# A fused seven-stage network on one core: later index products, two copies on ScalarE's DMA queue, a causal mask by addition, roots by log and exp, low weight parts on GpSimd, all in the sparse attention stage

## The chip, the cores and the metric

The kernel runs on one core of a Trainium2 chip. The core has a matrix engine (TensorE, PE in the profile), a vector engine (VectorE, DVE), an activation engine (ScalarE, ACT), a general engine (GpSimd, POOL) and a sequencer that here only starts transfers (SyncE, SP). Each engine takes its instructions strictly in program order; an instruction waits on semaphores for what it reads and for the buffer that it writes. ACT, POOL and SP can each start DMA transfers. The metric is the device time of one execution in microseconds (us), lower is better.

## The reference, cut to what matters

A sequence of 512 tokens with 1024 features goes through seven stages: ffn1, mix, ffn2, dsa, ffn3, conv, ffn4. Only dsa, a sparse attention, is touched here:

```python
proj = h @ w_in                       # q 16 heads, k and v 4 heads, qi 8 heads, ki 1, wi 8, head size 64
q = _rope(_rmsnorm(q, q_norm_g), positions);  k = _rope(_rmsnorm(k, k_norm_g), positions)
qi = _rope(qi, positions)
ki = _rope(_layernorm(ki, ...))       # one index key per token
# for each block of 128 queries:
score = einsum(relu(einsum(qi, ki)), wi * scale)      # sum over the 8 index heads
score = where(key <= query, score, -inf)              # causal
_, sel = top_k(score, 128)                            # 128 keys for each query
o = softmax(q . k[sel] * scale) . v[sel]
return o @ w_out
```

## The kernel before, in words

Every float32 matrix product is made of three products of rounded parts (high times high, high times low, low times high; L461 to L463). A weight tile is loaded by SP as `raw` (1 MB, L101), rounded by ACT to `whi` (L124, a cast of 128x1024), and its low part `wlo` is a subtraction (L126, 128x1024) by DVE, or by POOL for every second tile while `W.pool_lo` is true, and for every tile while it is 2. One projection of 128 output rows is a block of 24 matmuls.

The stage dsa_block runs so. First the index projections: ki with the 8 weights wi, then QI0 to QI3. Each goes through `rope`: `t` gets the halves of the raw tile swapped by DMAs of SP (L1464, L1465), POOL multiplies raw by cos (L1466) and t by sin (L1469), DVE adds (L1472). ki (tile U4, 64 partitions) is then copied to its upper 64 partitions by one DMA (L1525), since two index heads are computed at a time, one in each half of the array.

Next k0, k1, v0, v1 and q0 to q7 are projected, one block after the other. After each block stands a "step" (L470): it runs the functions that were put off (`deferred`), and one round of the generator `beside_q`. A round of it does, in this order: `weighed` (ACT's Relu of the last index products, L1567, and DVE's weighted sum over heads, L1569 and L1571; at head 7 the causal part by POOL's affine_select, L1575), `select` (rounds of top-8 search: MAX, L1605, and MATCH_REPLACE, L1606; 16 rounds for each query block j = 1, 2, 3, on 256, 384 and 512 columns), the sums of q's norms (`add`, L1681; its `rest` is DVE's L1686, POOL's power -0.5 in L1687 and four small POOL operations, L1689 to L1692), stages of attention "units", and `some_products` (the next index products on PE, L1555). `some_products` does nothing until `ready` is set, which `last` in evac_ki does by a deferred function.

A unit is a pair of heads of one set of query blocks: 8 units for j = 0 and 1, 8 for j = 2, 8 for j = 3. Its steps are scores (L1748), the masked reduction with the selection (DVE, L1765), Exp (ACT), division (DVE L1774, POOL L1776), transposes (PE L1785), copies (ACT L1796), values (PE L1807). When all q blocks are done a second loop runs the remaining units, one iteration each, with `select(1.4)` (two rounds) in each iteration while selection lasts. Units of j = 3 need sel[3], which one DVE instruction (L1609, 512 columns) writes when the 16 rounds of j = 3 are done.

DVE's and ACT's order is thus the order in which this Python code runs; nothing is rescheduled. Names of tiles: U4 ki, U0 to U3 the index queries, U14 to U21 q, F0 and F5 the raw k, F1 to F3 the index scores, `sq` the Relu results (two buffers), A and B the PSUM banks, `ada_w` q's raw tile, `col` small columns.

Of the kernel before, what the change touches and what calls it, by code (L numbers as in the profile page):

```python
# [18 lines left out]
P = 128  # L19
# [218 lines left out]
def body(ctx: ExitStack, tc: tile.TileContext, A: dict, consts: bass.AP, out: bass.AP,  # L238
# [1214 lines left out]
    def dsa_block(layer):  # L1453
# [5 lines left out]

        def rope(out, raw, n=P, then=None):  # L1460

            t = tmp()[0:n]
            for a in range(0, n, 64):
                nc.sync.dma_start(t[a:a + 32], raw[a + 32:a + 64])  # L1464
                nc.sync.dma_start(t[a + 32:a + 64], raw[a:a + 32])  # L1465
            nc.gpsimd.tensor_tensor(out, raw, cos[0:n], op=ALU.mult)  # L1466

# [20 lines left out]
        def evac_qi(c, ps):  # L1488
            raw = tmp()
            nc.scalar.copy(raw, ps)  # L1490
            rope(QI[c], raw)

# [3 lines left out]
        def evac_ki(c, ps):  # L1496
# [4 lines left out]
            def rest():  # L1501
# [11 lines left out]
                def more():  # L1513
# [10 lines left out]
                    def last():  # L1524
                        nc.sync.dma_start(ki[HALF[1]], ki[HALF[0]])  # L1525
                        deferred.append(lambda: ready.append(True))

                    rope(ki[HALF[0]], z, 64, last)

# [30 lines left out]
        def weighed():  # L1560

            for j, h, ps in parts:
# [5 lines left out]
                if h == 0:  # L1568
                    nc.vector.tensor_scalar(sc[:, 0:n], t[:, 0:n], w, None, op0=ALU.mult)  # L1569
                else:  # L1570
                    nc.vector.scalar_tensor_tensor(sc[:, 0:n], t[:, 0:n], w, sc[:, 0:n], op0=ALU.mult,  # L1571
                                                   op1=ALU.add)
                if h == 7:
                    dg = sc[:, P * j:n]
                    nc.gpsimd.affine_select(dg, dg, pattern=[[-1, P]], base=0, channel_multiplier=1,  # L1575
                                            compare_op=ALU.is_ge, fill=NEG)
                    whole.append(j)
# [50 lines left out]
        def evac_k(c, ps):  # L1628
# [4 lines left out]
            def swapped(t):  # L1633
                for i in range(2):
                    nc.sync.dma_start(KS[t][HALF[i]], kraw[t][HALF[1 - i]])

# [34 lines left out]
        def evac_q(c, ps):  # L1671
# [6 lines left out]
            def add():  # L1678
# [5 lines left out]
                def rest():  # L1684
                    v, y, z = colt((P, 8)), colt((P, 8)), colt((P, 8))
                    nc.vector.tensor_scalar(v, both, 1.0 / 64, EPS, op0=ALU.mult, op1=ALU.add)  # L1686
                    nc.gpsimd.tensor_tensor(y, v, mhalf, op=ALU.pow)  # L1687

# [175 lines left out]
        side_work.append(beside_q())  # L1864
        W.pool_lo = True
        proj_T("dsa", 2, H, evac_k)
        proj_T("dsa", 2, H, evac_v)
        proj_T("dsa", 8, H, evac_q)
        side_work.clear()
# [4 lines left out]
        go(1)  # L1874
        while adds:
            adds.pop(0)()
        phase[0] = False
        now = at[0]
        while at[6] < len(units):
            go(5, now - 4)  # L1880
            go(6)
            go(3, now - 2)
            go(0)
            go(2, now)
            now += 1
# [157 lines left out]
```

## Time and profile before

| | us |
|---|---|
| median of three runs (lowest to highest) | 2710.66 (2710.25 to 2711.5) |
| the profiled execution, its own time | 2706.65 |
| its span in the trace | 2704.9 |
| PE busy, share of the span | 2625.6, 97% |
| DVE busy | 1389.4, 51% |
| ACT busy | 908.7, 34% |
| POOL busy | 554.0, 20% |
| mean granted clock of PE | 0.985 |

The profile is of one execution. Busy time is that of instructions that do work; transfers and semaphores are not in it. A clock of 1.00 is 2.4 GHz, 0.50 is 1.2 GHz. The stage dsa covers about 1465 to 1740 us of the span.

### The profile page before, as it was taken

What the parts mean: (1) busy time and instruction counts of PE and PEld (TensorE: products, weight loads), DVE (VectorE), ACT (ScalarE), POOL (GpSimd) and SP (SyncE); (2) the same over time, 40 slices, a digit from 0 to 9 for tenths busy, and PEclk for the clock granted to TensorE, in tenths of its full rate; (3) what the DMA queues carried; (4) which work ended last, traced back from release to release, by engine and by line L of the source; (5) the groups of instructions that cost most, each with busy time, mean ns of one, the idle gap of its engine ahead of it and who ended that gap; (6) DMA issues with size and microseconds to landing.
All of it is one profiled execution on the core that took longest, in us unless ns stands there. A gap on an engine that the chain in (4) does not pass through costs nothing.

```text
span 2704.9 us, 32602 instructions
## 1 busy us (share of the span) xinstructions
PE 2625.6 (97%) x13020; PEld 2186.4 (81%) x13020; DVE 1389.4 (51%) x2060; ACT 908.7 (34%) x1447; POOL 554.0 (20%) x577
## 2 busy tenths in 40 slices
PE   8999999999999999999998787999999999999999
PEld 7888889888777788888887665888888888888887
DVE  5545566365637454665556587463333454533332
ACT  4322233323344433423223334642222332322222
POOL 3211234254112111412123346320000200200000
PEclk9999999999999999999999887999999999999999
DMA  6555443222221234256543221022232322232322
GB/s 186 160 177 184 150 144 115 63 78 79 85 72 63 78 100 135 90 156 201 184 147 123 75 74 59 2 93 91 97 109 71 117 94 94 79 105 82 109 86 71
DMA packets 256875, 289.11 MB, mean 107 GB/s; under 512 B 10004, under 2 KB 238916, under 8 KB 256724
## 3 DMA queue, kind: packets, MB, share of 16 engines
q1 hardware_dynamic: 244596, 235.57, 27.6%
q0 software_dynamic: 10496, 50.95, 6.0%
q8 instruction: 103, 1.69, 0.2%
q10 hardware_dynamic: 1632, 0.52, 0.1%
q14 instruction: 48, 0.39, 0.0%
HBM read 278.59 MB, written 4.19 MB: 105 GB/s over the span
## 4 chain that ended last, share of the span: by engine, by line
PE 88%; DVE 7%; POOL 1%; ACT 1%; issue 1%; DMA 1%; SPq 0%; DVEq 0%; ACTq 0%; POOLq 0%
PE mm L461 25%; PE mm L462 25%; PE mm L463 25%; PE mm L544 2%; PE mm L657 1%; PE mm L658 1%; PE mm L659 1%; DVE col L1605 1%; DVE F L1606 1%; PE B L1136 1%; DVE X L810 1%; DVE L L696 1%; PE mm L1748 1%; PE mm L1807 1%; PE A L1279 1%
## 5 line engine op out<-in xcount | busy, mean ns | idle before, releaser
L461 PE MATMUL mm<-H,whi 128*128 128x512 f32 (+1 forms) x2360 | 902.5, 382 | 0.0
L463 PE MATMUL mm<-H,wlo 128*128 128x512 f32 (+1 forms) x2360 | 894.1, 379 | 0.9 <-DVE wlo L126 0.9
L462 PE MATMUL mm<-L,whi 128*128 128x512 f32 (+1 forms) x2360 | 894.5, 379 | 0.3 <-DVE L L696 0.3
L126 DVE TENSOR_TENSOR wlo<-raw,whi 128x1024 fp32r<-128x1024 f32 (+3 forms) x432 | 503.6, 1166 | 547.8 <-ACT whi L124 546.1
L124 ACT CAST whi<-raw 128x1024 fp32r<-128x1024 f32 (+3 forms) x460 | 444.6, 968 | 408.8 <-PE mm L462 329.0
L461 PEld LDWEIGHTS mm<-H,whi 128*128 128x128 f32 x2360 | 445.9, 189 | 91.5 <-issue 10.7
L463 PEld LDWEIGHTS mm<-H,wlo 128*128 128x128 f32 x2360 | 445.4, 189 | 84.8 <-DVE wlo L126 1.6
L462 PEld LDWEIGHTS mm<-L,whi 128*128 128x128 f32 x2360 | 445.7, 189 | 82.1 <-DVE L L696 1.0
L461 PE MATMUL mm<-U,whi 128*128 128x512 f32 (+1 forms) x804 | 312.4, 389 | 0.0
L463 PE MATMUL mm<-U,wlo 128*128 128x512 f32 (+1 forms) x804 | 310.8, 387 | 0.0
L462 PE MATMUL mm<-U,whi 128*128 128x512 f32 (+1 forms) x804 | 310.7, 386 | 0.0
L413 POOL TENSOR_TENSOR acc<-acc,sq 128x512 f32<-128x512 f32 (+1 forms) x74 | 92.8, 1254 | 640.8 <-ACT sq L400 640.0
L670 ACT CAST U<-t 128x512 fp32r<-128x512 f32 x104 | 64.6, 621 | 406.9 <-POOL t L759 194.2
L461 PEld LDWEIGHTS mm<-U,whi 128*128 128x128 f32 x804 | 151.0, 188 | 33.5 <-issue 3.3
L463 PEld LDWEIGHTS mm<-U,wlo 128*128 128x128 f32 x804 | 151.0, 188 | 30.8
L462 PEld LDWEIGHTS mm<-U,whi 128*128 128x128 f32 x804 | 151.0, 188 | 30.1
L671 DVE TENSOR_TENSOR U<-t,U 128x512 fp32r<-128x512 f32 x104 | 72.0, 693 | 134.2 <-ACT U L670 134.2
L882 POOL DMA_DIRECT2D ada_w<-in_ada_w_dram x128 | 71.3, 557 | 281.1 <-DVE wide L906 221.1
L906 DVE SCALAR_TENSOR_TENSOR wide<-ada_w,csilu,wide 128x768 f32<-128x768 f32 x112 | 115.0, 1027 | 15.9 <-DMA ada_w<-in_ada_w_dram 15.9
L126 POOL TENSOR_TENSOR wlo<-raw,whi 128x1024 fp32r<-128x1024 f32 (+1 forms) x28 | 66.2, 2363 | 256.8 <-ACT whi L124 255.1
L757 DVE TENSOR_TENSOR t<-t,mm 128x512 f32<-128x512 f32 x88 | 60.3, 685 | 110.9 <-PE mm L463 110.8
L759 POOL TENSOR_TENSOR t<-t,R 128x512 f32<-128x512 f32 x44 | 56.4, 1283 | 217.5 <-DVE t L757 210.4
(394 smaller groups left out, 2807.9 us busy)
## 6 DMA issues: line engine op xcount, KB each, us to landing
ada_w<-in_ada_w_dram POOLq DMA_DIRECT2D x128, 384.0 KB, 3.6
raw<-in_ffn_w_up_dram SPq DMA_DIRECT2D x44, 1024.0 KB
raw<-in_ffn_w_gate_dram SPq DMA_DIRECT2D x43, 1024.0 KB
raw<-in_w_in_dram SPq DMA_DIRECT2D x30, 1024.0 KB
raw<-in_ffn_w_down_dram SPq DMA_DIRECT2D x32, 768.0 KB
raw<-in_ffn_w_down_dram SPq DMA_DIRECT2D x32, 640.0 KB
raw<-in_w_in_dram SPq DMA_DIRECT2D x24, 512.0 KB
raw<-in_conv_w_in_dram SPq DMA_DIRECT2D x12, 1024.0 KB
```

What stands on the lines that cost most here:

```text
L124: nc.scalar.copy(hi, raw)
L126: e.tensor_tensor(lo, raw, hi.bitcast(F32), op=ALU.subtract)
L413: (eng or nc.vector).tensor_tensor(self.acc[:, c], self.acc[:, c], sq[:, c], op=ALU.add)
L461: nc.tensor.matmul(ps, whi, hhi, start=start, stop=False)
L462: nc.tensor.matmul(ps, whi, hlo, start=False, stop=False)
L463: nc.tensor.matmul(ps, wlo, hhi, start=False, stop=stop)
L670: nc.scalar.copy(hi, src)
L671: nc.vector.tensor_tensor(lo, src, hi.bitcast(F32), op=ALU.subtract)
L757: nc.vector.tensor_tensor(s, s, ps, op=ALU.mult)
L759: nc.gpsimd.tensor_tensor(s, s, R, op=ALU.mult)
L882: nc.gpsimd.dma_start(loaded[i], A["ada_w_2"][layer, k * P:(k + 1) * P, 768 * cg:768 * (cg + 1)])
L906: nc.vector.scalar_tensor_tensor(acc, w, csilu[:, k:k + 1], acc, op0=ALU.mult, op1=ALU.add)
```

## The change

Eight edits, all in dsa_block:

1. `rope` takes an engine for the cos product. For the four index queries and ki it is DVE, before it was POOL.
2. ki's copy to the upper half is started from ACT's queue, before from SP's.
3. `ready` is set one step later, so all ten calls for index products come one projection block later.
4. The causal part is no longer POOL's affine_select after head 7. The first head's product is split: the columns before the diagonal block by a TENSOR_SCALAR, the 128 of the diagonal block by a SCALAR_TENSOR_TENSOR that also adds a triangular mask.
5. k's four half copies (`swapped`) are started from ACT's queue, before from SP's.
6. The power -0.5 of q's norms is ACT's Ln and Exp on 128x8, before one POOL operation.
7. While k and v are projected all low parts are made by POOL. Tiles are prepared ahead, so these are the weights of q0 to q3.
8. After the last projection the sum of q7's norm is taken up in the second loop, before it stood ahead of the loop.

```diff
-        def rope(out, raw, n=P, then=None):
+        def rope(out, raw, n=P, then=None, e=nc.gpsimd):
...
-            nc.gpsimd.tensor_tensor(out, raw, cos[0:n], op=ALU.mult)
+            e.tensor_tensor(out, raw, cos[0:n], op=ALU.mult)
...
-            rope(QI[c], raw)
+            rope(QI[c], raw, e=nc.vector)
...
-                        nc.sync.dma_start(ki[HALF[1]], ki[HALF[0]])
-                        deferred.append(lambda: ready.append(True))
+                        nc.scalar.dma_start(ki[HALF[1]], ki[HALF[0]])
+                        deferred.append(lambda: deferred.append(lambda: ready.append(True)))
-                    rope(ki[HALF[0]], z, 64, last)
+                    rope(ki[HALF[0]], z, 64, last, nc.vector)
...
-                    nc.vector.tensor_scalar(sc[:, 0:n], t[:, 0:n], w, None, op0=ALU.mult)
+                    nc.vector.tensor_scalar(sc[:, 0:P * j], t[:, 0:P * j], w, None, op0=ALU.mult)
+                    nc.vector.scalar_tensor_tensor(sc[:, P * j:n], t[:, P * j:n], w, masks[:, 896:1024], op0=ALU.mult,
+                                                   op1=ALU.add)
...
-                    dg = sc[:, P * j:n]
-                    nc.gpsimd.affine_select(dg, dg, pattern=[[-1, P]], base=0, channel_multiplier=1,
-                                            compare_op=ALU.is_ge, fill=NEG)
...
-                    nc.sync.dma_start(KS[t][HALF[i]], kraw[t][HALF[1 - i]])
+                    nc.scalar.dma_start(KS[t][HALF[i]], kraw[t][HALF[1 - i]])
...
-                    nc.gpsimd.tensor_tensor(y, v, mhalf, op=ALU.pow)
+                    act(y, v, AF.Ln)
+                    act(y, y, AF.Exp, scale=-0.5)
...
-        W.pool_lo = True
+        W.pool_lo = 2
         proj_T("dsa", 2, H, evac_k)
         proj_T("dsa", 2, H, evac_v)
+        W.pool_lo = True
         proj_T("dsa", 8, H, evac_q)
...
-        while adds:
-            adds.pop(0)()
         phase[0] = False
...
             go(0)
+            if adds:
+                adds.pop(0)()
+                banks.clear()
+                step()
             go(2, now)
```

Three places show how instructions move. The first is PE's order after the projection of k0 (matmuls into the tile `mm`); L1555 are the first index products, of ki (U_1184) with QI0 and QI1 (U_1180, U_1181). Before, they stand right behind k0, and k1 (mm_11407) follows:

```order
L462 MATMUL mm_11365<-L_1164_10900,whi_11231 128x512
L463 MATMUL mm_11365<-H_1163_10899,wlo_11232 128x512
L1555 MATMUL A_11392<-U_1184_10974,U_1180_10970 128x256 x2
L1555 MATMUL A_11392<-U_1184_10974,U_1181_10971 128x256 x2
L461 MATMUL mm_11407<-H_1149_10885,whi_11275 128x512
L462 MATMUL mm_11407<-L_1150_10886,whi_11275 128x512
```

Now the 24 matmuls of k1 (mm_11401) and the first sum of k's norms (L1659) stand ahead of them, and v0 (mm_11441) follows:

```order
L462 MATMUL mm_11401<-L_1164_10900,whi_11275 128x512
L463 MATMUL mm_11401<-H_1163_10899,wlo_11276 128x512
L1659 MATMUL B_11351<-acc_11393,dsa_consts 20x512
L1555 MATMUL A_11428<-U_1184_10974,U_1180_10970 128x256 x2
L1555 MATMUL A_11428<-U_1184_10974,U_1181_10971 128x256 x2
L461 MATMUL mm_11441<-H_1149_10885,whi_11302 128x512
L462 MATMUL mm_11441<-L_1150_10886,whi_11302 128x512
```

So PE has one block more to do before it needs ki's upper half and QI0, QI1. The second place is POOL from the start of the index queries' rotation on; `rc` is cos, `rs` sin, U_1180 to U_1183 the index queries, U_1184 ki. Before:

```order
L1466 TENSOR_TENSOR U_1180_10970<-t_11223,rc_8270 128x512
L1466 TENSOR_TENSOR U_1184_10974<-t_11260,rc_8270 64x512
L1469 TENSOR_TENSOR t_11225<-t_11225,rs_8271 128x512
L1466 TENSOR_TENSOR U_1181_10971<-t_11267,rc_8270 128x512
L1469 TENSOR_TENSOR t_11262<-t_11262,rs_8271 64x512
L1469 TENSOR_TENSOR t_11269<-t_11269,rs_8271 128x512
L1466 TENSOR_TENSOR U_1182_10972<-t_11294,rc_8270 128x512
L1469 TENSOR_TENSOR t_11296<-t_11296,rs_8271 128x512
L1466 TENSOR_TENSOR U_1183_10973<-t_11337,rc_8270 128x512
L1469 TENSOR_TENSOR t_11339<-t_11339,rs_8271 128x512
L126 TENSOR_TENSOR wlo_11455<-raw_11235,whi_11454 128x1024
L1575 AFFINE_SELECT F_1238_11393<-F_1238_11393 128x128
```

Now:

```order
L1469 TENSOR_TENSOR t_11225<-t_11225,rs_8271 128x512
L1469 TENSOR_TENSOR t_11262<-t_11262,rs_8271 64x512
L1469 TENSOR_TENSOR t_11269<-t_11269,rs_8271 128x512
L1469 TENSOR_TENSOR t_11296<-t_11296,rs_8271 128x512
L1469 TENSOR_TENSOR t_11339<-t_11339,rs_8271 128x512
L126 TENSOR_TENSOR wlo_11396<-raw_11235,whi_11395 128x1024
L126 TENSOR_TENSOR wlo_11438<-raw_11235,whi_11437 128x1024
L126 TENSOR_TENSOR wlo_11488<-raw_11306,whi_11487 128x1024
L126 TENSOR_TENSOR wlo_11571<-raw_11306,whi_11570 128x1024
```

The five cos products are gone from POOL, and four low parts stand right behind the last sin product, where one stood before. The third place is ACT after q2's block. Before, the Relu of the index scores (`sq`) follows the cast:

```order
L1673 ACTIVATE ada_w_11828<-mm_11755,cB 128x512
L1675 ACTIVATE acc_11830<-mm_11755 128x512
L124 CAST whi_11838<-raw_11529 128x1024
L1567 ACTIVATE sq_11886<-A_11822 128x512
L1567 ACTIVATE sq_11889<-A_11822 128x512
```

Now k's copies (U_1185, U_1186 from the raw k in F_1223, F_1224) and the Ln and Exp (on `col`) stand between them:

```order
L1672 ACTIVATE ada_w_11798<-mm_11743,cB 128x512
L1674 ACTIVATE acc_11800<-mm_11743 128x512
L124 CAST whi_11808<-raw_11491 128x1024
L1634 DMA U_1185_10975<-F_1223_11352 64x512 x2
L1634 DMA U_1186_10976<-F_1224_11353 64x512 x2
L364 ACTIVATE col_11847<-col_11846 128x8
L364 ACTIVATE col_11847<-col_11847 128x8
L1567 ACTIVATE sq_11857<-A_11793 128x384
L1567 ACTIVATE sq_11860<-A_11793 128x384
```

The Relu also works on 384 columns there (j = 2), where before it was at j = 3. Counts over the whole program: DVE 1983 rows before and 1989 after, ACT 1390 and 1409, POOL 582 and 568, SP 362 and 359, PE 11871 in both. ACT's rows hold 18 table loads in both. In DVE's order 8 of the 16 rounds of j = 3 stand ahead of the reduction of unit 4 (the last one while q is projected) before, 4 after; the instruction that writes sel[3] has 14 units' reductions behind it before, and 12 after.

## Rows read from the trace of the kernel before

**Rows 1.** The page: the span, the busy times, and PE's granted clock in 40 slices of the span (67.6 us each).

```profile
span 2704.9 us, 32602 instructions
...
PE 2625.6 (97%) x13020; PEld 2186.4 (81%) x13020; DVE 1389.4 (51%) x2060; ACT 908.7 (34%) x1447; POOL 554.0 (20%) x577
...
PEclk9999999999999999999999887999999999999999
```

**Rows 2.** Busy time by stretch: start and end, length, then busy us and count of PE, weight loads, DVE, ACT, POOL, then granted clock, DMA share, GB/s.

```profile
1524.00:1695.00 171.00, 126.01 (x631) 95.15 (x631) 123.83 (x294) 63.02 (x158) 85.64 (x109) 0.81 0.25 73
1695.00:1740.00 45.00, 45.00 (x470) 35.28 (x467) 24.61 (x92) 38.77 (x112) 19.21 (x31) 1.00 0.01 2
```

**Rows 3.** What PE waited for between 1524 and 1695 us: instruction that waited, what released it, us in total, times, longest.

```profile
PE B L1681 <- DVE col L1686: 13.0, 2, 10.8
PE A L1555 <- DMA U<-U: 7.9, 1, 7.9
PE B L1785 <- DVE col L1774: 6.8, 1, 6.8
PE B L1681 <- ACT U L1796: 6.0, 2, 4.3
PE A L1555 <- DVE U L1472: 5.3, 1, 5.3
PE mm L1748 <- DVE L L671: 4.2, 2, 2.9
```

**Rows 4.** A stretch of 10 us with the columns of rows 2.

```profile
1530.00:1540.00 10.00, 2.10 (x7) 1.17 (x6) 4.03 (x4) 0.00 (x0) 3.04 (x3) 0.50 0.75 221
```

**Rows 5.** The timeline around the first index products, of POOL, DVE, SP and PE: start, duration, engine, line, operation, out<-in, count, and in brackets the idle time before it and what ended it.

```profile
1518.90 2.14 POOL L1466 TENSOR_TENSOR U<-t,rc 64x512 f32<-64x512 f32 x1 [6.60 <-DVE t L1522]
1521.00 1.28 POOL L1469 TENSOR_TENSOR t<-t,rs 128x512 f32<-128x512 f32 x1
...
1527.67 2.35 DVE L1472 TENSOR_TENSOR U<-U,t 64x512 f32<-64x512 f32 x2
...
1531.93 0.58 SPq L101 DMA_DIRECT2D raw<-in_attn_w_in_dram  x1
1532.62 0.56 SPq L1525 DMA_DIRECT2D U<-U  x1
...
1539.44 1.26 POOL L1469 TENSOR_TENSOR t<-t,rs 128x512 f32<-128x512 f32 x1 [3.49 <-DMA t<-t]
...
1523.54 0.39 PE L462 MATMUL mm<-L,whi 128*128 128x512 f32 x1
1523.77 0.39 PE L463 MATMUL mm<-H,wlo 128*128 128x512 f32 x1
...
1538.60 2.07 PE L1555 MATMUL A<-U,U 64*128 64x256 f32 x6 [7.90 <-DMA U<-U]
```

**Rows 6.** POOL and DVE at one low part on POOL, and the same DVE operation a little earlier.

```profile
1549.55 2.40 POOL L126 TENSOR_TENSOR wlo<-raw,whi 128x1024 fp32r<-128x1024 f32 x1 [8.85 <-ACT whi L124]
...
1541.80 1.68 DVE L1571 SCALAR_TENSOR_TENSOR F<-sq,wcol,F 128x256 f32<-128x256 f32 x3
...
1549.82 2.40 DVE L1571 SCALAR_TENSOR_TENSOR F<-sq,wcol,F 128x256 f32<-128x256 f32 x1 [6.34 <-ACT sq L1567]
```

**Rows 7.** What DVE waited for between 1524 and 1695 us, the first three, with the columns of rows 3.

```profile
DVE F L1571 <- ACT sq L1567: 12.3, 5, 6.3
DVE U L1472 <- POOL t L1469: 10.3, 4, 3.6
DVE col L1605 <- POOL F L1575: 9.1, 3, 5.4
```

**Rows 8.** The timeline of POOL and DVE at the affine_select of j = 2.

```profile
1593.22 1.64 POOL L1687 TENSOR_TENSOR col<-col,mhalf 128x8 f32<-128x8 f32 x1
...
1597.17 0.29 POOL L1575 TENSOR_SCALAR_AFFINE_SELECT F<-F 128x128 f32<-128x128 f32 x1
...
1597.50 0.56 DVE L1605 MAX8 col<-F 128x8 f32<-128x384 f32 x1 [5.40 <-POOL F L1575]
```

**Rows 9.** Busy time from the second index products' sums to the end of unit 4's reduction, with the columns of rows 2.

```profile
1549.82:1663.50 113.68, 93.23 (x457) 71.99 (x455) 92.40 (x212) 41.05 (x96) 62.48 (x74) 0.86 0.26 75
```

**Rows 10.** Prices: groups of instructions of POOL and DVE between 1524 and 1695 us (line, engine, operation, tiles, count, busy us, mean ns, idle before), then two successive MAX of 512 columns in DVE's timeline.

```profile
L126 POOL TENSOR_TENSOR wlo<-raw,whi 128x1024 fp32r<-128x1024 f32 x6 | 14.8, 2469 | 20.1 <-ACT whi L124 20.0
...
L126 DVE TENSOR_TENSOR wlo<-raw,whi 128x1024 fp32r<-128x1024 f32 x8 | 11.5, 1434 | 1.6 <-ACT whi L124 1.6
...
1669.70 0.69 DVE L1605 MAX8 col<-F 128x8 f32<-128x512 f32 x1
...
1671.21 0.69 DVE L1605 MAX8 col<-F 128x8 f32<-128x512 f32 x1
```

**Rows 11.** DVE's timeline around the writing of sel[3]: the division that opens an iteration of the second loop, and L1609.

```profile
1689.35 0.17 DVE L1774 RECIPROCAL col<-col 128x4 f32<-128x4 f32 x1
...
1693.80 0.15 DVE L1774 RECIPROCAL col<-col 128x2 f32<-128x2 f32 x1
...
1694.93 0.65 DVE L1609 TENSOR_SCALAR U<-F 128x512 bf16<-128x512 f32 x1
...
1696.51 0.15 DVE L1774 RECIPROCAL col<-col 128x2 f32<-128x2 f32 x1
```

**Rows 12.** A small ACT instruction in its timeline.

```profile
1562.03 0.63 ACT L364 ACTIVATE wide<-t 4x512 f32<-4x512 f32 x1 [5.39 <-DVE t L1653]
```

## The prediction

> **What bounds the kernel now.** The first view is the page [rows 1]. PE is busy 97% of the span, so only a place where PE waits can be shortened. The granted clock falls below 9 tenths in three neighbouring slices only, the 23rd to the 25th of 40, about 1490 to 1690 us. That is the stage dsa. The second view, busy time by stretch [rows 2], says how much lies there: from 1524 to 1695 us PE is busy 126.0 of 171.0 us, at a mean clock of 0.81; from 1695 on it is busy without a gap at 1.00. So 45.0 us of waiting and some loss by the clock lie in these 171 us, and what happens after 1695 us only shifts with them.
>
> The third view is PE's list of waits in this stretch [rows 3]. Two of them, 5.3 and 7.9 us, are one gap: the first index products wait for the index key ki (DVE's addition L1472), then for its copy to the upper half. Beside this gap the clock is 0.50 [rows 4]. The rest, 13.0, 6.8, 6.0 and 4.2 us, are waits for DVE, directly or through ACT. DVE is busy 123.8 of the 171 us [rows 2]. It is therefore the engine that sets the pace, and the fourth view is what DVE itself waits for [rows 7]: Relu results of ACT (12.3 us), POOL's rotation products (10.3 us), POOL's affine_select (9.1 us).
>
> The timeline at the second j shows what the last one is [rows 8]: the affine_select takes 0.29 us, but POOL starts it at 1597.17 behind the power (1593.22, 1.64 us) and others, and DVE's search, 1597.50, has stood 5.40 us.
>
> The end of the chain is sel[3]. It is written at 1694.93 [rows 11], and from there on PE has no gap [rows 2]. So the question is when sel[3] comes, and how much PE has still to do then.
>
> **The change part by part.**
>
> *The first gap.* POOL no longer does ki's cos product (2.14 us) nor that of QI0 or QI1 (one by one as long as the sin product, 1.28 us) ahead of ki's sin product [rows 5]. The addition of ki, which ends about 1529.4 (1527.67 plus most of 2.35), comes about 2.14 + 1.28 = 3.4 us earlier, at 1526.0. DVE takes the five products at prices like its other two-input sums, 0.56 us for 256 columns [rows 6], in time in which it stands. The copy was issued at 1532.62, behind the 1 MB load at 1531.93, and its wait ended at 1538.60, 6.0 us after [rows 5]. From ACT's queue it goes out at 1526.0, ahead of that load. Its flight was not seen without the load; it lies between its issue, 0.56 us, and 6.0 us, so it lands at 1526.6 to 1532.0. Meanwhile PE does k1: 24 matmuls 0.23 us apart [rows 5] are 5.5 us, from 1524.1 to 1529.6. The 13.2 us gap shrinks to 0 to 2.4 us; I take 0, as the load that made the flight long now comes later.
>
> *A new wait one block on.* The second products need QI3. SP starts its swaps behind those of QI2, which wait for ki's addition, so they come 3.4 us earlier too: the sin product at 1539.44 [rows 5] moves to 1536.0 and ends at 1537.3. Behind it on POOL now stand two low parts of 2.4 us [rows 6]. DVE's addition for QI3 ends between 1538 (not hindered) and 1542.1 (both in the way). PE has finished v0 by 1529.6 + 1.0 + 5.5 = 1536.1 (the products took 2.07 us at half clock), and waits 2 to 6 us. DVE then has four sums (4 x 0.56), the root for k's norms (four instructions on 4x512, taken like ACT's at 0.63 us [rows 12], and two on ACT), 2.2 + 2.5 + 1.3 = 6.0 us, so its second sums start between 1544 and 1548, and up to 3 us later if the low parts stretch them too. Before they began at 1549.82 [rows 6]. I take no shift; the ends are 6 us earlier and 1 us later. So most of PE's gain at the first gap does not reach DVE.
>
> *DVE from there to unit 4.* Before, this is 1549.82 to 1663.50: 113.7 us, of which DVE works 92.4 and stands 21.3 [rows 9]. In the changed order the same stretch holds 4 rounds of j = 3 fewer (1.51 us each by the distance of two MAX [rows 10], 6.0 us), one low part fewer (1.4 us [rows 10]), the four root instructions fewer (2.5 us), and two mask sums more (at most 0.56 each, 1.1 us). That leaves 92.4 - 6.0 - 1.4 - 2.5 + 1.1 = 83.6 us. Of the standing time the 9.1 us for the affine_select go [rows 7]: 12.2 us are left. Of these, 12.3 - 6.3 = 6.0 are waits for the Relu, which stay. I take 9 us, the middle of 6.0 and 12.2, because POOL is freed of eight powers of 1.64 us [rows 8] and of five cos products, while ACT gets 16 small instructions, at most 16 x 0.63 = 10 us [rows 12], in 171 us of which it works 63 [rows 2]. The stretch takes 92.6 us, 21.1 less.
>
> *What is given back.* The search is later: 12 rounds instead of 8 are left for the second loop, six iterations with two rounds instead of four. An iteration with rounds lasts 4.45 us (1689.35 to 1693.80), one without 2.71 (1693.80 to 1696.51) [rows 11]. Two more cost 2 x 1.74 = 3.5 us. The units themselves are no more: sel[3] has two units fewer behind it.
>
> *Without a term.* k's copies on ACT's queue: four issues of 0.56 us [rows 5], 2.2 us on ACT, hidden in its idle time; if ACT stands there for DVE, what is behind it is the Relu, and that is a rival below. q7's sum taken up in the loop moves one short DVE pair, nothing.
>
> The sum: 0 + 21.1 - 3.5 = 17.6 us less. On the profiled execution's own time that is 2706.65 - 17.6 = 2689.1. The median of the runs is 4.0 us above that execution, so the forecast is 2710.66 - 17.6 = 2693 us.
>
> **A rule that speaks against the change.** DVE's sum of 256 columns took 2.40 us while POOL made a low part of 2.40 us, against 0.56 us alone [rows 6]. The Trainium skill, "GPSIMD Engine Reference", section "Key points", says that the engine shares its SBUF interfaces with VectorE and contends with instructions that have two SBUF inputs. Rows 6 bear it out for this kind. By the rows alone, with 1.4 us of DVE's time saved for a low part moved, the term stands as in the sum; by the rule a low part moved to POOL relieves DVE of nothing when it has two-input work just then, and the sum is that of the first rival.
>
> **The rivals.**
>
> *The port.* Each of the four low parts on POOL stretches a DVE sum by 2.40 - 0.56 = 1.84 us, 7.4 us in all; nothing of this is in the sum from 1549.8 on. For it: they stand together behind the last sin product, at the sums of j = 1. Against: the search takes one input, and before its end DVE stood anyway. The gain is 10.2 us, 2700 us. Chance 0.12.
>
> *The gaps nearly all go.* The second sums start 6 us earlier, and DVE stands 6.0 us where I took 9: 17.6 + 6 + 3 = 26.6 us, 2684; if it does not stand at all, 32.6 us, 2678. For it: PE's first gap goes in full. Against: DVE's sums need PE, ACT and DVE in turn, and 6.0 us of that were there before. Chance 0.13.
>
> *The copy stays late.* The ki copy waits on ACT behind a cast, or flies 6 us in spite of its place. Then the first gap keeps up to 8 us, of which DVE sees 5: 12.6 us, 2698. Chance 0.10.
>
> *A new wait takes the old one's place.* Now ACT's Ln waits for DVE's L1686, with the Relu of the index scores behind it on ACT, and DVE's sums wait for the Relu. If this costs what the affine_select cost (9.1 us) and the 3.2 us that I took off beside it, the gain is 17.6 - 12.3 = 5 us, 2705. Chance 0.10.
>
> *Slower: ACT held at each of the eight steps with q.* The same place, but a full round trip each time: DVE ends its search rounds, does L1686, ACT does k's copies or Ln and Exp, then Relu, then DVE sums. The nearest price for DVE standing before an in-order engine is 9.1 us in three waits [rows 7], 3.0 each. Eight of these are 24 us, 6 us slower than before: 2717. It decides above (17.6 + 5.4) / 8 = 2.9 us for each step. For it: ACT's order puts Ln ahead of the Relu. Against: L1686 stands ahead of the sums in DVE's order too, and the 63 us that ACT works in 171 leave room. Chance 0.10.
>
> That the change does nothing at all would need the affine_select's 9.1 us to come back and the first gap to stay; it lies within the last two.
>
> **How the numbers follow.** The forecast has 0.45, with its own range of 2687 to 2698. With 0.12 + 0.13 + 0.10 and a little of the 2705 case on the faster side, faster by over 0.2% (5.4 us, about what a measurement of this kernel can tell from no change) has 0.82; within 0.2% 0.08; slower 0.10. The range from 2678 to 2706 leaves out the slower case and a little at either end.
>
> **What would show it.** In the changed profile PE's first index products (L1555) start by 1532 and the gap there is under 3 us; a gap of 2 to 6 us stands before the second ones, about 1536 to 1543. No MAX waits for POOL. From the second sums to the end of unit 4 about 93 us pass, and sel[3] comes about 1682 to 1683, with 12 units behind it, each 2.7 us. It is wrong if DVE's waits for the Relu are well over 12 us, or if PE stands long in the second loop because 12 rounds are left.

## The result and the profile after

The changed kernel takes 2690.38 us (median of four runs, 2688.74 to 2691.53); the kernel before, run beside it, takes 2711.08 (2710.25 to 2713.86). The ratio is 0.9921, with an interval of 0.9904 to 0.9939: 20.7 us less, where 17.6 were forecast.

The page of the changed kernel, with the lines of [rows 1]: PE's busy time is the same, and the span is shorter by waits.

```profile
span 2688.6 us, 32606 instructions
...
PE 2627.9 (98%) x13020; PEld 2188.0 (81%) x13020; DVE 1388.2 (52%) x2066; ACT 910.9 (34%) x1463; POOL 539.5 (20%) x563
```

One thing has to be taken out before rows are compared. Ahead of the changed code the two profiled executions already differ. The last product of dsa's input norm on PE, in before and in after:

```profile
1494.91 0.71 PE L452 MATMUL B<-cst,col 128*128 128x128 f32 x4 [0.35 <-DVE col L444]
...
1500.11 0.71 PE L452 MATMUL B<-cst,col 128*128 128x128 f32 x4 [0.34 <-DVE col L444]
```

It starts 5.2 us later in after, with the same instructions ahead of it; over all 14 traces of this document it lies between 1494.4 and 1501.3. All times of after below are 5.2 us later on the clock for that reason, and "from the norm" means from this row of the same trace. From the norm to the end before took 2704.9 - 1494.91 = 1210.0 us and after 2688.6 - 1500.11 = 1188.5 us, 21.5 us less, which fits the medians (20.7).

What PE waited for (1524 to 1690 us), against [rows 3]: the two waits of 5.3 and 7.9 us for ki are gone, that of 10.8 us for q's norm is 2.1 at most, that of 6.8 us for the division 1.1. New are 5.2 us for a Relu and 6.6 us for a copy of ACT.

```profile
PE mm L1748 <- ACT U L1818: 6.6, 1, 6.6
PE A L1555 <- ACT sq L1567: 5.2, 1, 5.2
PE mm L1748 <- DVE L L671: 4.1, 2, 2.7
PE B L1680 <- DVE col L1685: 3.4, 2, 2.1
...
PE B L1785 <- DVE col L1774: 1.1, 1, 1.1
```

The first index products in the timeline, against [rows 5]: ki's addition (64 partitions) on DVE, the copy from ACT's queue, the products without a wait in brackets; then the second products, the late sin product of QI3, two low parts on POOL, and the two DVE instructions beside them.

```profile
1530.55 0.68 DVE L1472 TENSOR_TENSOR U<-U,t 64x512 f32<-64x512 f32 x1
...
1531.26 0.56 ACTq L1525 DMA_DIRECT2D U<-U  x1
...
1535.70 1.13 PE L1555 MATMUL A<-U,U 64*128 64x256 f32 x8
...
1548.69 2.08 PE L1555 MATMUL A<-U,U 64*128 64x256 f32 x8 [5.19 <-ACT sq L1567]
...
1540.94 1.29 POOL L1469 TENSOR_TENSOR t<-t,rs 128x512 f32<-128x512 f32 x1 [4.44 <-DMA t<-t]
1542.19 5.09 POOL L126 TENSOR_TENSOR wlo<-raw,whi 128x1024 fp32r<-128x1024 f32 x2
...
1542.27 2.81 DVE L1472 TENSOR_TENSOR U<-U,t 128x512 f32<-128x512 f32 x1 [5.04 <-POOL t L1469]
1545.01 2.36 DVE L1569 TENSOR_SCALAR F<-sq,wcol 128x128 f32<-128x128 f32 x1
```

The stretch of [rows 9], from the second sums to the end of unit 4's reduction, and the one from there to the writing of sel[3], in after:

```profile
1554.40:1648.57 94.17, 80.42 (x425) 63.64 (x425) 79.19 (x198) 39.23 (x102) 51.27 (x64) 0.91 0.27 79
1648.57:1683.86 35.29, 29.32 (x182) 21.55 (x181) 28.93 (x95) 18.83 (x67) 13.47 (x32) 0.71 0.10 30
```

And in before the second of them, which [rows 9] does not hold:

```profile
1663.50:1694.93 31.43, 20.11 (x132) 14.93 (x133) 20.57 (x69) 13.05 (x49) 14.40 (x30) 0.69 0.11 34
```

What DVE waited for in after (1524 to 1690 us), against [rows 7]: no search waits for POOL any more.

```profile
DVE U L1472 <- POOL t L1469: 11.0, 4, 5.0
DVE F L1573 <- ACT sq L1567: 9.0, 5, 2.4
DVE L L671 <- ACT H L670: 4.0, 4, 1.2
```

DVE's work changed too, and not only by what the edits move. The stretch to unit 4 holds the same 18 weighted sums over heads in both kernels, with 384, 512 and 256 columns. The groups of that stretch with their busy us and mean ns, first before (1549.82 to 1663.50), then after (1554.40 to 1648.57): 22.9 us in all against 14.6.

```profile
L1571 DVE SCALAR_TENSOR_TENSOR F<-sq,wcol,F 128x384 f32<-128x384 f32 x7 | 10.4, 1493 | 1.8 <-ACT sq L1567 1.4
L1571 DVE SCALAR_TENSOR_TENSOR F<-sq,wcol,F 128x512 f32<-128x512 f32 x7 | 8.6, 1225 | 5.0 <-ACT sq L1567 4.6
L1571 DVE SCALAR_TENSOR_TENSOR F<-sq,wcol,F 128x256 f32<-128x256 f32 x4 | 3.9, 965 | 6.7 <-ACT sq L1567 6.3
...
L1573 DVE SCALAR_TENSOR_TENSOR F<-sq,wcol,F 128x512 f32<-128x512 f32 x7 | 6.8, 974 | 6.4 <-ACT sq L1567 6.0
L1573 DVE SCALAR_TENSOR_TENSOR F<-sq,wcol,F 128x384 f32<-128x384 f32 x7 | 5.9, 840 | 3.4 <-ACT sq L1567 3.0
L1573 DVE SCALAR_TENSOR_TENSOR F<-sq,wcol,F 128x256 f32<-128x256 f32 x4 | 1.9, 481 | 0.3
```

The long ones of before stand beside an operation of POOL with two inputs, as in [rows 6]. One more of them, from before:

```profile
1587.76 2.36 POOL L126 TENSOR_TENSOR wlo<-raw,whi 128x1024 fp32r<-128x1024 f32 x1
...
1588.05 4.05 DVE L1571 SCALAR_TENSOR_TENSOR F<-sq,wcol,F 128x384 f32<-128x384 f32 x2 [1.41 <-ACT sq L1567]
```

The 21.5 us are thus four differences: the second sums start 0.6 us earlier from the norm (54.3 against 54.9), the stretch to unit 4 takes 19.5 us less (94.2 against 113.7), that to sel[3] 3.9 us more (35.3 against 31.4), and from sel[3] to the end it is 5.2 us less (1004.7 against 1010.0), since two units fewer are left.

### The profile page after: what moved, and what is told of

Same layout as the page of the kernel before. It is cut to its first block, busy times and chain, and to the rows that moved or that the text cites. A ratio compares the mean times of both kernels' runs of the same rounds, so it can differ in the third digit from the quotient of the medians.

```text
span 2688.6 us, 32606 instructions
## 1 busy us (share of the span) xinstructions
PE 2627.9 (98%) x13020; PEld 2188.0 (81%) x13020; DVE 1388.2 (52%) x2066; ACT 910.9 (34%) x1463; POOL 539.5 (20%) x563
## 4 chain that ended last, share of the span: by engine, by line
PE 88%; DVE 8%; ACT 1%; POOL 1%; issue 1%; DMA 1%; SPq 0%; ACTq 0%; DVEq 0%; POOLq 0%
PE mm L461 25%; PE mm L462 25%; PE mm L463 25%; PE mm L544 2%; PE mm L657 1%; PE mm L658 1%; PE mm L659 1%; DVE F L1605 1%; DVE col L1604 1%; PE B L1136 1%; DVE X L810 1%; DVE L L696 1%; PE A L1279 1%; PE B L1302 1%; PE mm L1807 1%
## 5 line engine op out<-in xcount | busy, mean ns | idle before, releaser
L413 POOL TENSOR_TENSOR acc<-acc,sq 128x512 f32<-128x512 f32 (+1 forms) x74 | 92.4, 1248 | 642.1 <-ACT sq L400 641.4
L126 POOL TENSOR_TENSOR wlo<-raw,whi 128x1024 fp32r<-128x1024 f32 (+1 forms) x30 | 71.8, 2396 | 246.7 <-ACT whi L124 245.1
```

The costliest lines, as they stand in the source:

```text
L126: e.tensor_tensor(lo, raw, hi.bitcast(F32), op=ALU.subtract)
L413: (eng or nc.vector).tensor_tensor(self.acc[:, c], self.acc[:, c], sq[:, c], op=ALU.add)
```

## The experiments

Two theories went in. DVE's pace: the end follows the writing of sel[3], and a wait of PE counts only as far as it makes DVE late. The gap: what PE waits at the first index products is the gain. The names of the runs begin with u where one edit is undone in the changed kernel, with b where one or some are made in the kernel before, with x where something new is tried.

All of them by the same four pieces, in us. "Work" and "stands" are DVE's in the stretch from the second sums to unit 4. The times from the norm are of one profiled execution each; the medians are of 4 to 11 runs, that of before is of the 21 runs taken beside the experiments. How well a piece repeats can be seen where two kernels have the same code: up to unit 4 before and b_adds differ by 0.1 us at most, after and u_adds by 0.5.

| kernel | second sums, from the norm | to unit 4 (DVE works, stands) | to sel[3] | to the end | from the norm to the end | median |
|---|---|---|---|---|---|---|
| before | 54.9 | 113.7 (92.4, 21.3) | 31.4 | 1010.0 | 1210.0 | 2710.3 |
| b_cos | 52.3 | 113.4 (92.1, 21.3) | 31.0 | 1010.0 | 1206.6 | 2706.4 |
| b_ready | 60.2 | 98.6 (80.9, 17.7) | 39.9 | 1006.3 | 1205.0 | 2705.1 |
| b_front | 53.1 | 97.3 (79.6, 17.7) | 40.3 | 1004.7 | 1195.4 | 2695.8 |
| b_adds | 54.8 | 113.7 (92.4, 21.3) | 28.1 | 1010.0 | 1206.5 | 2707.8 |
| after | 54.3 | 94.2 (79.2, 15.0) | 35.3 | 1004.7 | 1188.5 | 2690.4 |
| u_ready | 48.9 | 103.6 (88.4, 15.2) | 26.4 | 1010.0 | 1188.9 | 2689.3 |
| u_mask | 54.0 | 96.4 (79.3, 17.1) | 35.3 | 1004.7 | 1190.4 | 2690.3 |
| u_adds | 54.1 | 94.7 (79.8, 14.9) | 40.8 | 1004.7 | 1194.3 | 2694.6 |
| u_root | 54.2 | 92.4 (80.5, 11.9) | 37.0 | 1004.7 | 1188.3 | 2689.1 |
| u_queues | 54.5 | 93.1 (79.1, 14.0) | 35.3 | 1004.7 | 1187.5 | 2691.3 |
| x_roots | 54.3 | 93.3 (81.6, 11.7) | 33.2 | 1004.6 | 1185.4 | 2687.6 |
| x_lo2 | 54.2 | 91.9 (77.3, 14.6) | 35.3 | 1004.9 | 1186.3 | 2686.7 |
| x_best | 53.8 | 93.3 (81.3, 12.0) | 33.2 | 1004.7 | 1185.0 | 2685.4 |

**u_ready**

```diff
-                        deferred.append(lambda: deferred.append(lambda: ready.append(True)))
+                        deferred.append(lambda: ready.append(True))
```

> The changed kernel with one edit undone: ready is set one step earlier again, so the first index products stand behind k0's block, not behind k1's. Theory of DVE's pace: PE gets a gap of 4 to 7 us at the first products, waiting for ki's addition and its copy, but DVE gets its sums and search rounds a block earlier, and 8 rounds instead of 12 are left for the second loop; the time stays within 5 us of the changed kernel, 2686 to 2696. Rival, the gap is the gain: what PE waits at the first products comes out at the end, 5 us or more slower, 2696 to 2703.

2689.29 us, ratio 0.9931 (0.9918 to 0.9943) to before, not told apart from the changed kernel. PE waits again at the first products, for ki's addition and its copy:

```profile
PE A L1555 <- DMA U<-U: 2.0, 1, 2.0
PE A L1555 <- DVE U L1472: 1.9, 1, 1.9
```

and it costs nothing: DVE's second sums start 5.4 us earlier, four rounds more lie in the stretch to unit 4 (103.6), four fewer behind it (26.4), and two units more are left after sel[3]. DVE's pace holds here. With the other seven edits made, setting `ready` later is neutral.

**u_queues**

```diff
-                        nc.scalar.dma_start(ki[HALF[1]], ki[HALF[0]])
+                        nc.sync.dma_start(ki[HALF[1]], ki[HALF[0]])
...
-                    nc.scalar.dma_start(KS[t][HALF[i]], kraw[t][HALF[1 - i]])
+                    nc.sync.dma_start(KS[t][HALF[i]], kraw[t][HALF[1 - i]])
```

> The changed kernel with the copy of ki and the copies of k started from SP's queue again. The copy of ki then stands behind the swaps of QI2 and a 1 MB load and lands some 5 us later, so PE waits about 5 us at the first index products. Theory of DVE's pace: DVE's sums of j = 1 wait for QI3's rotation anyway, and the time stays, 2688 to 2693. Rival, the gap is the gain: 5 us slower, 2694 to 2698.

2691.32 us, ratio 0.9924 (0.9912 to 0.9936). PE waits 3.8 us for the copy and the end does not move, as DVE's second sums wait for QI3 anyway (54.5 against 54.3):

```profile
PE A L1555 <- DMA U<-U: 3.8, 1, 3.8
```

QI3's sin product starts 40.9 us from the norm, in the changed kernel 40.8. So in the changed kernel either of the two can be undone without a loss, the copy from ACT's queue or the block put ahead. Both undone together was not run.

**b_front, b_ready and b_cos**

```diff
# b_front: edits 1, 2 and 3 in the kernel before.  b_ready: edit 3 alone.  b_cos: edit 1 alone.
-            rope(QI[c], raw)
+            rope(QI[c], raw, e=nc.vector)
...
-                        nc.sync.dma_start(ki[HALF[1]], ki[HALF[0]])
-                        deferred.append(lambda: ready.append(True))
+                        nc.scalar.dma_start(ki[HALF[1]], ki[HALF[0]])
+                        deferred.append(lambda: deferred.append(lambda: ready.append(True)))
-                    rope(ki[HALF[0]], z, 64, last)
+                    rope(ki[HALF[0]], z, 64, last, nc.vector)
```

> The kernel before with three of the edits alone: cos on DVE, ki's copy on ACT's queue, ready one step later. Theory of DVE's pace: PE's 13.2 us gap closes, but DVE's second sums start no earlier and its waits for POOL's affine_select (9.1 us) stay; of the stretch to unit 4 only the 4 rounds and the root's four instructions leave, 8.5 us, and 3.5 us are given back: 5 us faster than before, 2702 to 2708. Rival, the gap is the gain: 13 us faster or more, 2693 to 2698.

> The kernel before with one edit alone: ready one step later. k1's block moves ahead of the first index products; the copy of ki still lands at 1538.5, so PE's gap of 13.2 us becomes about 9. If what counts is the block that is put ahead (PE has k1 and v0 done when the index products come, and four rounds of the search move from the stretch with q to the second loop), the time is within 4 us of that with all three front edits (2695.8): 2692 to 2700. Rival, the gap counts: 4 us faster than before only, 2704 to 2708.

> The kernel before with one edit alone: the cos products of the index queries and of ki on DVE. ki's addition and its copy come 3.4 us earlier, the copy still behind the load; the first gap shrinks to about 10 us and all else stays: 2706 to 2709. Rival: what POOL is freed of lets QI1 to QI3 come earlier too and is most of the front's gain: 2698 to 2704.

b_front 2695.77 us, ratio 0.9952 (0.9940 to 0.9965); b_ready 2705.08, 0.9983 (0.9974 to 0.9991); b_cos 2706.36, 0.9986 (0.9978 to 0.9995). By the times, b_front and b_ready came out where the gap theory had them, 14 and 5 us faster, and only b_cos where I put it. The stretches of b_front say that the way was another:

```profile
1553.82:1651.15 97.33, 79.89 (x416) 62.45 (x414) 79.60 (x196) 37.72 (x91) 62.89 (x73) 0.89 0.26 76
1651.15:1691.47 40.32, 28.74 (x184) 21.37 (x185) 29.11 (x93) 17.69 (x63) 16.68 (x34) 0.68 0.09 27
```

The second sums start only 1.8 us earlier. The stretch to unit 4 falls by 16.4 us, from 113.7 to 97.3, where I had worked out 8.5; the next grows by 8.9, and two units fewer are left (5.3 us). In the stretch to unit 4 DVE works 12.8 us less and stands 3.6 less. Rounds (5.9), three of the root's instructions (2.1) and a low part (1.6) had left it, as expected; the weighted sums over heads, which I had not counted, take 15.5 us, 7.4 less than before, against 4.3 more in the additions of the rotation (L1472) and the writing of sel[1] and sel[2]. The search's waits for POOL, which I had taken to stay, are 6.3 us in place of 9.1.

b_ready has nearly the same stretches (98.6 and 39.9) but starts them 7.1 us later than b_front, and its first products wait 7.6 us for the copy:

```profile
PE A L1555 <- DMA U<-U: 7.6, 1, 7.6
```

Of the 7.1 us, 3.7 are there at DVE's first sums already: they follow QI3's sin product, which starts 44.7 us from the norm in b_ready, with the cos products on POOL, and 41.0 in b_front. Both rows, b_ready's first:

```profile
1543.07 1.26 POOL L1469 TENSOR_TENSOR t<-t,rs 128x512 f32<-128x512 f32 x1 [3.59 <-DMA t<-t]
...
1541.76 1.28 POOL L1469 TENSOR_TENSOR t<-t,rs 128x512 f32<-128x512 f32 x1 [4.60 <-DMA t<-t]
```

The other 3.4 us come between the first and the second sums, where DVE waits 4.1 us for a weight's cast (0.7 in b_front), which on ACT stands behind the copy of the v0 block that PE, late by its wait, has just ended. So neither theory holds as it was put: in the kernel before the gain of the later `ready` lies in DVE's stretch to unit 4, and half of it is lost again at the start where ki and QI3 do not come earlier as well. How much of that is the copy's queue alone is not shown: ki's copy alone on ACT's queue was not run.

**u_mask**

```diff
-                    nc.vector.tensor_scalar(sc[:, 0:P * j], t[:, 0:P * j], w, None, op0=ALU.mult)
-                    nc.vector.scalar_tensor_tensor(sc[:, P * j:n], t[:, P * j:n], w, masks[:, 896:1024], op0=ALU.mult,
-                                                   op1=ALU.add)
+                    nc.vector.tensor_scalar(sc[:, 0:n], t[:, 0:n], w, None, op0=ALU.mult)
...
+                    dg = sc[:, P * j:n]
+                    nc.gpsimd.affine_select(dg, dg, pattern=[[-1, P]], base=0, channel_multiplier=1,
+                                            compare_op=ALU.is_ge, fill=NEG)
```

> The changed kernel with POOL's affine_select back and the mask sum gone. If the affine_select's place on POOL was what cost DVE 9.1 us, the search waits for POOL again, three waits of 1 to 5 us, and the time goes up by 5 to 9 us, 2695 to 2699. Rival: the power and the cos products were what stood ahead of it on POOL; with these gone the waits are under 1 us each, and the time stays, 2689 to 2692.

2690.33 us, ratio 0.9931 (0.9919 to 0.9944), the rival's time. The three waits of the search for POOL are 2.2 us in all, one of them over 1 us, against 9.1 [rows 7]:

```profile
DVE col L1605 <- POOL F L1575: 2.2, 3, 1.4
```

What DVE had stood for was mostly not the affine_select (0.29 us) but what POOL had ahead of it. The mask edit's own share is some 2 us: from the norm to the end u_mask takes 1.9 us more than the changed kernel, which the medians do not show. Which of POOL's work it was is known in part. The cos products, which the rival named, had no share: in b_cos, without them, the three waits are still 9.1 us. With `ready` later they are 6.2 (b_ready) and 6.3 (b_front). The rest goes with the edits that u_mask has beyond b_front, the power's among them; these were not tested one by one with the affine_select in place.

**u_root and x_roots**

```diff
# u_root
-                    act(y, v, AF.Ln)
-                    act(y, y, AF.Exp, scale=-0.5)
+                    nc.gpsimd.tensor_tensor(y, v, mhalf, op=ALU.pow)
# x_roots: Ln, Exp and the four POOL operations in a function that the step calls later
+                    def root():
                        act(y, v, AF.Ln)
                        act(y, y, AF.Exp, scale=-0.5)
...
+                    roots.append(root)
...
                 if parts:
                     weighed()
+                while roots:
+                    roots.pop(0)()
```

> The changed kernel with the power back on POOL in place of ACT's Ln and Exp. Theory of ACT's hold, from the changed trace: at 1647.34 ACT's Ln has stood 6.87 us for DVE's L1685, the copy of a unit's output (L1818) stands behind it, and PE waits 6.63 us for that copy; without Ln and Exp this wait goes and the time falls by 2 to 6 us, 2684 to 2689. Rival: PE's wait there costs nothing, since DVE sets the pace, and the power (1.6 us, eight times) makes POOL later: 2690 to 2694.

> The changed kernel with Ln and Exp (and the four POOL operations behind them) issued later in the same step: behind the copies, the divisions' Exp and the Relu on ACT, not ahead of them. Theory of ACT's hold: PE's wait of 6.6 us for the copy L1818 goes, and part of DVE's 9.0 us for the Relu; 2683 to 2688. Rival, DVE sets the pace and PE's wait is in its shadow: 2689 to 2692.

The wait that both are about, in the changed kernel: DVE's norm at 1647.15, ACT's Ln that had stood 6.87 us for it, the copy behind the Ln, and PE.

```profile
1647.15 0.15 DVE L1685 TENSOR_SCALAR col<-B 128x8 f32<-128x8 f32 x1
...
1647.34 0.45 ACT L364 ACTIVATE col<-col 128x8 f32<-128x8 f32 x2 [6.87 <-DVE col L1685]
1647.69 0.35 ACT L1818 COPY U<-mm 128x256 f32<-128x256 f32 x1
...
1648.10 0.58 PE L1748 MATMUL mm<-U,U 64*128 64x128 f32 x1 [6.63 <-ACT U L1818]
```

u_root 2689.11 us, ratio 0.9919 (0.9907 to 0.9932): between the two expectations. DVE stands 3.1 us less in the stretch to unit 4 (11.9 against 15.0), but the next stretch is 1.7 us longer, and the time from the norm to the end is the same (1188.3 and 1188.5). x_roots 2687.61 us, ratio 0.9914 (0.9902 to 0.9926): PE's wait for L1818 is gone (PE waits 8.0 us for a reduction of DVE instead), and it is 3.1 us shorter from the norm to the end. So the place where the edit puts Ln and Exp costs about 3 us against a later one. That this is ACT's hold is argued, not shown: in u_root PE's wait for that copy is gone too, and nothing is gained. The medians alone, 2.8 us apart with overlapping intervals, do not show it.

**u_adds and b_adds**

```diff
# u_adds (b_adds is the same in the other direction, in the kernel before)
+        while adds:
+            adds.pop(0)()
         phase[0] = False
...
             go(0)
-            if adds:
-                adds.pop(0)()
-                banks.clear()
-                step()
             go(2, now)
```

> The changed kernel with q7's norm sum taken up ahead of the second loop again. The prediction gave this edit no time: then 2689 to 2692. Rival, from the changed trace, where the time from the end of unit 4's reduction to the writing of sel[3] is 35.2 us for six iterations with rounds, and 40.3 us was worked out from the four before: this edit saves about 5 us, and without it the time is 2694 to 2698.

> The kernel before with one edit alone: q7's norm sum is taken up in the second loop. If this edit is worth the 5 us that its undoing cost in the changed kernel, by taking away PE's wait of 6.8 us for the division (L1785 for L1774), the time is 2702 to 2706. Rival: it is worth that only where 12 rounds are left for the second loop, and here it is 2708 to 2711.

u_adds 2694.58 us, ratio 0.9950 (0.9936 to 0.9964): 4.2 us are lost, and the stretch from unit 4 to sel[3] is 40.8 us in place of 35.3. b_adds 2707.79, ratio 0.9990 (0.9982 to 0.9999): between the two expectations; its stretch is 28.1 us in place of 31.4. Where the time lies, in u_adds, is the reductions of the first units of the second loop on DVE, which wait for their scores:

```profile
1650.14 0.35 DVE L1765 CUSTOM_DVE_ANT_0 t<-mm,masks,R 128x128 f32<-128x128 f32 x1 [1.58 <-PE mm L1748]
...
1660.01 0.35 DVE L1765 CUSTOM_DVE_ANT_0 acc<-mm,masks,R 128x128 f32<-128x128 f32 x1 [3.20 <-PE mm L1748]
```

In the changed kernel the same two have no wait:

```profile
1652.48 0.32 DVE L1765 CUSTOM_DVE_ANT_0 t<-mm,masks,R 128x128 f32<-128x128 f32 x1
...
1658.47 0.32 DVE L1765 CUSTOM_DVE_ANT_0 acc<-mm,masks,R 128x128 f32<-128x128 f32 x1
```

1.58 + 3.20 = 4.8 us. The edit does not move DVE's two instructions only. It puts the scores of the next unit ahead of the sums on PE, which is the first wait. The second one starts at PE's transposes into bank B, which the scores stand behind; u_adds, then the changed kernel:

```profile
1656.88 1.51 PE L1785 MATMUL B<-cst,U 128*128 128x128 f32 x6 [6.77 <-DVE col L1774]
...
1652.63 1.51 PE L1785 MATMUL B<-cst,U 128*128 128x128 f32 x6 [1.09 <-DVE col L1774]
```

q7's sums lie in bank B too, and DVE's L1685, which reads them, starts 0.08 us ahead of the division L1774 in both. In u_adds the two stand behind two rounds of the search, in the changed kernel ahead of them. So PE waited for that pair of DVE; which of the two held it is not shown.

**x_lo2**

```diff
-        W.pool_lo = True
+        W.pool_lo = 2
         proj_T("dsa", 8, H, evac_q)
+        W.pool_lo = True
```

> The changed kernel with all low parts on POOL while q is projected too, four more than now. Rows: each takes 1.2 to 1.4 us from DVE and can stretch a two-input operation of DVE by 1.84 us. If the stretch falls on DVE each time, the time goes up by 1 to 3 us, 2690 to 2693. Rival: DVE's search, which is not stretched, runs meanwhile, and DVE is relieved of 5 us: 2684 to 2688.

2686.67 us, ratio 0.9916 (0.9902 to 0.9930). The rival's time holds, its 5 us of relief do not: DVE works 77.3 us in the stretch to unit 4 against 79.2, and the stretch takes 91.9 against 94.2. The four low parts that leave DVE took 5.9 us there in the changed kernel; 1.9 are freed, so 4.0 were given back, most of it by the weighted sums over heads (18.7 us against 14.6): 1.0 for each low part, not 1.84.

**x_best**

```diff
# on top of x_roots
-            rope(QI[c], raw, e=nc.vector)
+            rope(QI[c], raw, e=nc.vector, q=nc.scalar if c == 3 else nc.sync)
...
-                nc.sync.dma_start(t[a:a + 32], raw[a + 32:a + 64])
+                q.dma_start(t[a:a + 32], raw[a + 32:a + 64])
```

> The changed kernel with the later Ln and Exp and with QI3's half swaps started from ACT's queue, ahead of the 1 MB load that they now follow on SP's. In the changed kernel DVE stands 5.0 us for QI3's sin product, and its second sums start only then. DVE's pace: they start 3 to 4 us earlier and the end follows; with the 2.8 us of the later Ln and Exp 2682 to 2686. Rival: the four issues hold ACT 2.3 us and make its casts late, or the later search rounds eat the lead: 2687 to 2691.

2685.41 us, ratio 0.9912 (0.9899 to 0.9926), in the expected range, but not by the expected way. DVE's second sums start 0.5 us earlier than in x_roots, not 3 to 4, and from the norm to the end there is 0.4 us between the two. PE's wait for the Relu (5.2) is gone, and one for ACT's square of k stands in its place, since the four issues hold ACT:

```profile
PE B L1659 <- ACT acc L1630: 3.6, 1, 3.6
```

The version is 3.5 us shorter than the changed kernel from the norm to the end, most of it by x_roots, and it is the fastest that was run; by the medians' intervals the two are not told apart. x_roots together with x_lo2 was not run.

## Why the prediction was right

**The first gap** (0 us taken): ki's addition ends at 1531.2, which is 1526.0 on before's clock, the value worked out; the copy goes out at once, and the first products do not wait.

**The new wait one block on** (2 to 6 us): 5.19 us, at 1548.69, 1543.5 on before's clock. The size was right, the path is longer than was said. The products did not wait for QI3 itself: its addition ends at 1545.08, 1539.9 on before's clock and within the 1538 to 1542.1 worked out. They waited for a Relu, which waits for DVE's first sums, and these stand behind that addition:

```profile
1547.72 0.38 ACT L1567 ACTIVATE sq<-A 128x256 f32<-128x256 f32 x1 [9.53 <-DVE F L1570]
```

DVE's second sums start 0.6 us earlier, where no shift was taken. That is partly luck. From QI3's addition to the second sums 6.0 us were worked out and 9.3 passed, since two more instructions of DVE were held beside POOL (2.36 us at 1545.01, and 1.70 us in the root); the number came from taking the late end of the range.

**DVE to unit 4** (92.6 us): 94.2. Both its terms were off and nearly cancel, which is luck too. DVE works 79.2 us, not 83.6, and stands 15.0, not 9. What was named came about as sized: rounds 5.9 us (6.0 taken), the low part 1.1 (1.4), the root 2.1 (2.5; one of its four instructions stayed). What had no term is the weighted sums over heads, 8.3 us less, against 3.8 more in the additions of the rotation and the writing of sel[1]. The standing was under-sized: waits for the Relu are 10.5 us (9.0 and 1.5 for the first product), not 6.0, one for a weight's cast is 1.0, and short gaps of about 3.5 in all make up the rest. The wait of about 5 us for QI3's product lies just ahead of the stretch.

**The affine_select** (9.1 us taken off): the waits did go, but u_mask shows that only some 2 us of them go by the mask edit once POOL is freed otherwise. The step put most of these 9.1 us to the wrong edit, and the sum was right because it counted it once.

**What is given back** (3.5 us): two iterations more and two units fewer came as worked out: in u_adds, without edit 8, the stretch from unit 4 to sel[3] is 40.8 us, where the working gives 31.4 + 2 x 4.45 = 40.3. An iteration with rounds has not changed:

```profile
1678.28 0.16 DVE L1774 RECIPROCAL col<-col 128x2 f32<-128x2 f32 x1
...
1682.73 0.15 DVE L1774 RECIPROCAL col<-col 128x2 f32<-128x2 f32 x1
1683.86 0.64 DVE L1608 TENSOR_SCALAR U<-F 128x512 bf16<-128x512 f32 x1
...
1685.43 0.15 DVE L1774 RECIPROCAL col<-col 128x2 f32<-128x2 f32 x1
```

4.45 and 2.70 us, as in [rows 11].

**q7's sum** ("moves one short DVE pair, nothing"): this step failed. It is worth 4.2 us by the medians and 5.8 from the norm to the end (u_adds), 3.5 in the kernel before (b_adds). The pair was the point: PE waited for it, and the wait is the one of 6.8 us for the division in [rows 3], to which the prediction gave no price. This is more than the forecast is short (3.1 us by the medians): sel[3] and the units behind it came out 4.8 us better than forecast, the second sums 0.6 better, the stretch to unit 4 1.6 worse.

**The rivals.** The port: DVE instructions were held beside the low parts, but mostly ahead of the second sums, and in the stretch to unit 4 DVE works less than forecast, not more; x_lo2 is faster with four more low parts on POOL, so no loss. The gaps nearly all go: the second sums start 0.6 us earlier, not 6, and DVE stands more than was taken, not less. The late copy: u_queues shows that it would not have counted in this kernel. ACT's hold: ACT does stand long for DVE's norm, but what comes of it is at most about 3 us (x_roots), not the 24 of the slower rival; that DVE mostly has rounds to do meanwhile is the likely reason, not tested by itself.

**What was wrong behind a right number**: the largest single term was the wait for the affine_select (9.1 us), and the front was thought to be worth 5 us (the expectation for b_front). Edits 1 to 3 alone have 14.6 of the 21.5 us from the norm to the end, the wait for the affine_select among them only in part. What the working lacked is that a later `ready` also changes what DVE's sums coincide with on POOL. That they take less time is measured; that the coinciding is the whole reason is argued from the rows. Edit 7 alone, the four low parts of the k and v blocks, was not undone in any run.

## What to carry to other kernels

A long wait for a short instruction can be a wait for what stands ahead of it on the same engine: look at that engine's queue before the instruction is replaced. Where one engine sets the pace, ask of every wait of another engine whether it moves the next start on the first one, and count what the first one works as well: the same 18 sums took 22.9 us in one order and 14.6 in another. And when a piece of code moves in a loop, list what it moves past on every engine: here a short pair of DVE that came to stand ahead of two search rounds, and scores that came to stand ahead of sums on PE, were worth 4 to 6 us.

## What the runs showed of the hardware

DVE instructions with one input can be held beside POOL too. The TENSOR_SCALAR on 128 columns at 1545.01 took 2.36 us beside POOL's two low parts, where the same one took 0.27 in u_ready, with POOL idle, and one on 256 columns 0.34 in before. This fits the rule of the Trainium skill, "GPSIMD Engine Reference", section "Key points", which names DVE's 2-port mode beside two SBUF inputs; no run here shows in which mode the instruction ran. It does not decide the time: with four more low parts on POOL DVE gave back 1.0 us for each, about half of the 1.84 in [rows 6], and 5.9 us of low parts had left it.
